# Scores of both context query tiles of a head in one run of matmuls, in the halves of two PSUM banks

## The chip, the cores and the metric

One NeuronCore of a Trainium2 chip runs the whole program. The metric is device time in microseconds of one execution, as the median of several runs. Engines are named as in the profile: PE is TensorE (PEld its weight loads), DVE is VectorE, ACT is ScalarE, POOL is GpSimd, SP is SyncE, which issues the large transfers.

## The reference

Two layers work on 256 latent tokens and 256 context tokens of width 2048. Each layer projects both streams with one wide matrix, runs differential attention and a chunked gating MLP side by side, merges them under sigmoid gates and projects the result. The part that matters here is the attention, with 8 heads, two score maps m per head, and 64 elements in each query and key:

```python
def _pair_attend(q, k, v):
    s = jnp.einsum('bqhmd,bkhmd->bhmqk', q, k).astype(jnp.float32) * (A_QK_DIM ** -0.5)
    p = jax.nn.softmax(s, axis=-1).astype(v.dtype)
    return jnp.einsum('bhmqk,bkhe->bqhme', p, v)
```

The latent queries attend to all 512 keys. The context queries attend to the 256 context keys only, and only in the first of the two layers, since the last layer's context output is not used.

## The kernel before

All matrices are multiplied in three passes of a high and a low part (`mm3`), so each float32 product is three matmuls. The tokens are four tiles of 128: tiles 0 and 1 are context, 2 and 3 latent. The large work is a sequence of chunks of 512 output columns (`tok_chunk`, `tok_steps`, line 315). A chunk loops over pairs of 128 input rows, inside over the token tiles, and each tile has its own PSUM bank of the four tagged `mm`. At the end of a chunk each tile's bank is copied out by a small task, which needs a `w2` buffer first (seven of them, 128 x 512), and the next chunk's first matmul needs a bank that has been copied out.

Everything else runs as Python generators that are interleaved with the chunks when the program is built. The builder keeps a clock of its own (`now`) and the times at which buffers come free (`pool`), and after every few large matmuls it calls `tick` (line 195). `tick` goes through the tasks in the order in which they were made and lets each go on whose request is met: `pe=1` asks for PE (one such step in a tick), `ms=2` for two of the four small PSUM banks, `w2=2` for two buffers, `cond` for a condition. The order that comes out is kept on every engine (lines 47 and 48 for DVE, ACT and POOL, line 231 for matmuls, line 238 for transposes), so most rows of the profile carry one of these three lines. The semaphores behind it are made by the framework, which keeps two engines from touching one PSUM bank at once.

Attention is one task per head and side, `attend` (line 849). `sd == 1` is the latent side with 512 keys, `sd == 0` the context side with 256. Each task takes two query tiles q one after the other. For a tile it asks for two `ms` banks and computes two 128 x nkt score maps with six matmuls: three passes, each over both maps, where map 0 contracts over partitions 0 to 63 and map 1 over partitions 64 to 127. Then come two maxima on DVE, two exponentials on ACT, after each of which a bank is given back, the weighted difference on DVE, a transposition through another `ms` bank and the split into high and low. After both tiles the product with the values is taken (6 matmuls on the context side, 12 on the latent side), in turn (`done["turn"]`, line 904). The counter `done["s"]` (lines 857 and 858) makes the score runs of all tasks come in one fixed order: latent tile 0, latent tile 1, context tile 0, context tile 1, then the next head. So a head's first score run cannot start before the second context run of the head before it was made. The tasks of a pair of heads are made behind the chunk with its queries and keys (lines 1059 to 1066); its two `s8` buffers are given back with the last context run of the pair (line 867).

Of the kernel before, what the change touches and what calls it, by code (L numbers as in the profile page):

```python
# [16 lines left out]
P = 128  # L17
# [4 lines left out]
QKD = 64  # L22
# [340 lines left out]
def dit_kernel(ctx, tc, x, c, ctxt, c_ctx, w_ada, b_ada, norm_g, w_in, q_norm_g, k_norm_g,  # L363
# [3 lines left out]
    B = Builder(ctx, tc)  # L367
# [380 lines left out]
    def layer(L, xt, xn_ev, x_in=None):  # L748
        last = L == DEPTH - 1
# [97 lines left out]
        done = {"n": 0, "turn": 0, "s": 0}  # L847

        def attend(st, vbox, hd, sd, order):
            i = hd % 2  # L850
            es = slice((hd % 4) * P, (hd % 4 + 1) * P)
            vs = slice(i * P, (i + 1) * P)
            nk = 4 if sd == 1 else 2
            nkt = nk * P
            ds = []
            for q in range(2):
                yield dict(pe=1, ms=2, w2=2, cond=lambda: st["n"] == 4 and done["s"] == 2 * order + q)
                done["s"] += 1
                qq, kk = st["qk"]
                ts = slice((2 * sd + q) * P, (2 * sd + q + 1) * P)  # L860
                S = [B.ms()[:, :nkt] for _ in range(2)]
                for a, b in ((0, 0), (0, 1), (1, 0)):
                    for m in range(2):
                        ms_ = slice(m * QKD, (m + 1) * QKD)
                        B.matmul(S[m], qq[ms_, a, i, ts], kk[ms_, b, i, 0:nkt], a + b == 0, a == 1)
                if q == 1 and i == 1 and (sd == 0 or last):
                    B.rel("s8", 2)
                nm = B.st()
                sm = B.st()
                Ps = []  # L870
                for m in range(2):
                    yield
                    V.tensor_reduce(out=nm[:, m:m + 1], in_=S[m], axis=AX.X, op=ALU.max, negate=True)
                for m in range(2):
                    yield
                    p = B.w2()
                    A.activation(out=p[:, :nkt], in_=S[m], func=AF.Exp, bias=nm[:, m:m + 1], scale=1.0,
                                 accum_out=sm[:, m:m + 1])
                    B.rel("ms")
                    Ps.append(p)  # L880
                yield
                rc = B.st()
                V.reciprocal(out=rc[:, 0:2], in_=sm[:, 0:2])
                V.tensor_tensor(out=rc[:, 1:2], in0=rc[:, 1:2], in1=nlam[:, L:L + 1], op=ALU.mult)
                V.tensor_scalar(out=Ps[1][:, :nkt], in0=Ps[1][:, :nkt], scalar1=rc[:, 1:2], scalar2=None, op0=ALU.mult)
                yield
                V.scalar_tensor_tensor(out=Ps[0][:, :nkt], in0=Ps[0][:, :nkt], scalar=rc[:, 0:1], in1=Ps[1][:, :nkt],
                                       op0=ALU.mult, op1=ALU.add)
                B.rel("w2")
                ds.append(Ps[0])  # L890
                if q == 0:
                    yield dict(pe=1, ms=1, cond=lambda: done["turn"] == order and vbox["n"] == 4,
                               **(dict(ws=2) if sd == 1 else dict(w2=2)))
                    dt = [B.t("ws" if sd == 1 else "w2", [P, nk, 256], F32R) for _ in range(2)]
                else:
                    yield dict(pe=1, ms=1)
                pt = B.transpose4([ds[q][:, b * P:(b + 1) * P] for b in range(nk)])
                B.rel("w2")
                yield
                qs = slice(q * P, (q + 1) * P)  # L900
                yield from B.hl(dt[0][:, :, qs], dt[1][:, :, qs], pt[:, :nkt].rearrange("p (b q) -> p b q", q=P))
                B.rel("ms")
            yield dict(pe=1, ms=1, w2=1)
            done["turn"] += 1
            v = vbox["v"][(hd // 2) % 2]
            po = B.ms()
            for kt in range(nk):
                B.mm3(po[:, 0:256], v[:, 0, kt, vs], v[:, 1, kt, vs], dt[0][:, kt], dt[1][:, kt], kt == 0, kt == nk - 1)
            B.rel("ws" if sd == 1 else "w2", 2)
            if i == 1 and (sd == 0 or last):  # L910
                B.rel("s8")
            yield
            dT = B.w2()
            A.copy(out=dT[:, 0:256], in_=po[:, 0:256])
            B.rel("ms")
            yield dict(pe=1, ms=1, **(dict(s8=1) if dn[hd // 4] is None else {}))
            if dn[hd // 4] is None:
                dn[hd // 4] = B.t("s8", [P, nq, 512])
            pq = B.transpose4([dT[:, 0:P], dT[:, P:2 * P]])
            yield  # L920
            ssd = B.st()
            for q in range(2):
                A.activation(out=dT[:, 256 + q * P:256 + (q + 1) * P], in_=pq[:, q * P:(q + 1) * P], func=AF.Square,
                             accum_out=ssd[:, q:q + 1])
            B.rel("w2")
            yield
            box = []
            yield from B.rstd(box, ssd[:, 0:2], 2, P)
            for q in range(2):
                V.tensor_scalar(out=dn[hd // 4][:, 2 * sd + q - q0, es], in0=pq[:, q * P:(q + 1) * P],  # L930
                                scalar1=box[0][:, q:q + 1], scalar2=None, op0=ALU.mult)
            B.rel("ms")
            done["n"] += 1
# [3 lines left out]
        def spawn_pair(st, vbox, p):  # L937
            nonlocal nunit
            for hd in (2 * p, 2 * p + 1):
                for sd in ((1,) if last else (1, 0)):  # L940
                    B.spawn(attend(st, vbox, hd, sd, nunit))
                    nunit += 1
# [540 lines left out]
```

## Time and profile before

| what | value |
|---|---|
| median of 3 runs | 2314.8 us (2314.11 to 2315.73) |
| the profiled execution, its own time | 2314.04 us |
| its span, first to last instruction | 2312.3 us |
| PE busy | 2271.8 us (98%), 10730 matmuls |
| DVE busy | 1487.3 us (64%) |
| ACT busy | 881.1 us (38%) |
| HBM traffic | 377.04 MB read, 5.24 MB written |
| TensorE clock granted, mean | 1.000 |

Busy times are unions of the intervals of an engine's instructions. A matmul's interval reaches past the start of the next one, so what a matmul costs is read from the distance between two starts and not from its duration. Windows are in microseconds from the span's start. In a timeline, neighbouring instructions of one kind are merged into one row with their count.

### The profile page before, as it was taken

Reading aid. Unit: us, or ns where it says so; the run is one execution under the profiler, and the core shown is the slowest. Engines: PE = TensorE matmul, PEld = TensorE weight load, DVE = VectorE, ACT = ScalarE, POOL = GpSimd, SP = SyncE. Lnnn points to the kernel's source line nnn. Section 1 sums busy time; section 2 is a strip of 40 time slices with the busy share of each in tenths; the row PEclk is TensorE's granted clock in tenths of the full one; section 3 lists DMA queues with packets and bytes.
Section 4 is the critical chain, followed back from the end, with each engine's and each line's share of the span. In section 5 each row is a group of like instructions: output and inputs, shape, how many; then the busy total and the mean of one; then the engine's idle time right before and its main releaser. Section 6 shows DMA issues by size and latency. Waiting matters only on the chain.

```text
span 2312.3 us, 28445 instructions
## 1 busy us (share of the span) xinstructions
PE 2271.8 (98%) x10730; PEld 1834.7 (79%) x10730; DVE 1487.3 (64%) x2343; ACT 881.1 (38%) x1387; POOL 112.7 (5%) x119
## 2 busy tenths in 40 slices
PE   4999999999999999999999999999999999999999
PEld 1577777778888888878888888888888888888887
DVE  3456666664446667687766766877757766677655
ACT  3234444452332212223222322554545554444443
POOL 2010111110000000000000000000201000000000
PEclk9999999999999999999999999999999999999999
DMA  9952222333335555555555566654334567777765
GB/s 330 351 174 73 82 74 73 87 92 106 99 91 166 160 157 165 171 167 166 172 160 157 157 206 196 188 162 130 100 92 140 171 186 247 256 252 255 251 201 182
DMA packets 230649, 384.15 MB, mean 166 GB/s; under 512 B 14446, under 2 KB 80080, under 8 KB 229744
## 3 DMA queue, kind: packets, MB, share of 16 engines
q1 hardware_dynamic: 228640, 377.56, 52.4%
q0 software_dynamic: 1872, 4.78, 0.9%
q8 instruction: 84, 1.38, 0.2%
q14 instruction: 53, 0.43, 0.1%
HBM read 377.04 MB, written 5.24 MB: 165 GB/s over the span
## 4 chain that ended last, share of the span: by engine, by line
PE 95%; DMA 3%; DVE 1%; ACT 0%; issue 0%; SPq 0%; DVEq 0%; ACTq 0%
PE mm L231 87%; PE ms L231 4%; PE ms L238 3%; DMA s<-in_w_ada_dram 1%; DMA raw<-in_w_ada_dram 1%; DMA s<-in_x_dram 1%; DVE wl L47 0%; DMA raw<-in_w_in_dram 0%; DMA ws<-in_w_ada_dram 0%; DVE ws L47 0%; DVE w L47 0%; ACT w L47 0%; DVE s L47 0%; DVE x L47 0%; SPq L275 0%
## 5 line engine op out<-in xcount | busy, mean ns | idle before, releaser
L231 PE MATMUL mm<-wh,x 128*128 128x512 f32 (+1 forms) x4352 | 1378.6, 389 | 1.3 <-DVE w L47 1.0
L231 PEld LDWEIGHTS mm<-wh,x 128*128 128x128 f32 x4352 | 810.0, 188 | 189.7 <-issue 30.2
L47 DVE TENSOR_TENSOR wl<-raw,wh 128x1024 fp32r<-128x1024 f32 x496 | 606.6, 1223 | 457.6 <-ACT wh L47 456.1
L47 ACT CAST wh<-raw 128x1024 fp32r<-128x1024 f32 x496 | 521.3, 1052 | 920.0 <-PE mm L231 677.9
L231 PE MATMUL mm<-wl,x 128*128 128x512 f32 (+1 forms) x2176 | 835.2, 384 | 1.2 <-DVE wl L47 1.2
L231 PEld LDWEIGHTS mm<-wl,x 128*128 128x128 f32 x2176 | 409.8, 188 | 74.5 <-DVE wl L47 2.0
L231 PE MATMUL mm<-x,wh 128*128 128x512 f32 x1024 | 316.1, 390 | 0.0
L47 DVE SCALAR_TENSOR_TENSOR ws<-raw,c,ws 128x512 f32<-128x512 f32 x420 | 288.2, 747 | 13.7 <-DMA raw<-in_w_ada_dram 13.0
L231 PEld LDWEIGHTS mm<-x,wh 128*128 128x128 f32 x1024 | 191.7, 188 | 39.9
L231 PE MATMUL mm<-x,wl 128*128 128x512 f32 x512 | 199.5, 390 | 0.0
L231 PE MATMUL mm<-s,wh 128*128 128x512 f32 x512 | 157.8, 389 | 0.0
L47 POOL TENSOR_TENSOR st<-st,c 128x8 f32<-128x8 f32 (+3 forms) x76 | 91.3, 1208 | 877.5 <-DVE st L47 875.6
L231 PEld LDWEIGHTS mm<-x,wl 128*128 128x128 f32 x512 | 96.1, 188 | 20.1
L231 PEld LDWEIGHTS mm<-s,wh 128*128 128x128 f32 x512 | 96.1, 188 | 20.1
L47 DVE TENSOR_REDUCE st<-ms 128x1 f32<-128x512 f32 (+2 forms) x104 | 56.0, 566 | 71.8 <-PE ms L238 40.9
L231 PE MATMUL mm<-s,wl 128*128 128x512 f32 x256 | 99.8, 390 | 0.9 <-DVE wl L47 0.9
L231 PE MATMUL ms<-s,s 64*128 64x512 f32 (+2 forms) x412 | 72.6, 461 | 18.1 <-DVE st L47 12.7
L238 PE MATMUL ms<-c,w 128*128 128x128 f32 (+1 forms) x466 | 74.4, 273 | 13.0 <-DMA w<-in_k_norm_g_dram 6.6
L238 PEld LDWEIGHTS ms<-c,w 128*128 128x128 f32 (+1 forms) x466 | 57.4, 141 | 32.5 <-issue 6.8
L231 PE MATMUL mm<-wh,s 128*128 128x512 f32 x256 | 81.6, 391 | 0.0
L47 ACT ACTIVATE w<-mm 128x512 f32<-128x512 f32 x72 | 43.0, 598 | 98.9 <-PE mm L231 98.8
L47 ACT ACTIVATE w<-ms,st 128x512 f32<-128x512 f32 (+1 forms) x96 | 58.6, 616 | 50.5 <-DVE st L47 50.5
(112 smaller groups left out, 1335.3 us busy)
## 6 DMA issues: line engine op xcount, KB each, us to landing
raw<-in_w_in_dram SPq DMA_DIRECT2D x296, 512.0 KB, 4.0
raw<-in_w_ada_dram SPq DMA_DIRECT2D x128, 512.0 KB, 4.5
raw<-in_w_out_dram SPq DMA_DIRECT2D x72, 512.0 KB, 4.4
raw<-in_w_in_dram SPq DMA_DIRECT2D x128, 256.0 KB, 3.0
raw<-in_w_proj_b_dram SPq DMA_DIRECT2D x32, 512.0 KB, 4.6
raw<-in_w_proj_a_dram SPq DMA_DIRECT2D x32, 512.0 KB, 4.5
s<-in_w_ada_dram SPq DMA_DIRECT2D x62, 256.0 KB, 6.0
raw<-in_w_ada_dram SPq DMA_DIRECT2D x38, 256.0 KB, 6.0
```

The costliest lines, as they stand in the source:

```text
L47: ins = getattr(self.eng, name)(**kw)
L231: self.tc.keep_in_program_order(self.nc.tensor.matmul(out=out, lhsT=lhsT, rhs=rhs, start=start, stop=stop))
L238: self.tc.keep_in_program_order(self.nc.tensor.transpose(out=out, in_=in_, identity=identity))
```

## The change

On the context side (`sd == 0`) the request for PE and two banks is made once. All twelve score matmuls of both query tiles are issued without a break: the six of tile 0 into the first 256 columns of the two banks, then the six of tile 1 into the last 256. The score counter goes up by two at that point, and the `s8` buffers of the pair are given back there. For tile 1 only the request for two `w2` buffers is left, which needs no PE. The banks are given back after the exponentials of tile 1 alone. The latent side issues what it did.

```diff
             ds = []
+            both = sd == 0
             for q in range(2):
-                yield dict(pe=1, ms=2, w2=2, cond=lambda: st["n"] == 4 and done["s"] == 2 * order + q)
-                done["s"] += 1
-                qq, kk = st["qk"]
-                ts = slice((2 * sd + q) * P, (2 * sd + q + 1) * P)
-                S = [B.ms()[:, :nkt] for _ in range(2)]
-                for a, b in ((0, 0), (0, 1), (1, 0)):
-                    for m in range(2):
-                        ms_ = slice(m * QKD, (m + 1) * QKD)
-                        B.matmul(S[m], qq[ms_, a, i, ts], kk[ms_, b, i, 0:nkt], a + b == 0, a == 1)
-                if q == 1 and i == 1 and (sd == 0 or last):
-                    B.rel("s8", 2)
+                if both and q == 1:
+                    yield dict(w2=2)
+                else:
+                    yield dict(pe=1, ms=2, w2=2, cond=lambda: st["n"] == 4 and done["s"] == 2 * order + q)
+                    qq, kk = st["qk"]
+                    banks = [B.ms() for _ in range(2)]
+                    qs_ = (0, 1) if both else (q,)
+                    done["s"] += len(qs_)
+                    for q_ in qs_:
+                        ts = slice((2 * sd + q_) * P, (2 * sd + q_ + 1) * P)
+                        ks = slice(q_ * nkt, q_ * nkt + nkt) if both else slice(0, nkt)
+                        for a, b in ((0, 0), (0, 1), (1, 0)):
+                            for m in range(2):
+                                ms_ = slice(m * QKD, (m + 1) * QKD)
+                                B.matmul(banks[m][:, ks], qq[ms_, a, i, ts], kk[ms_, b, i, 0:nkt], a + b == 0, a == 1)
+                    if qs_[-1] == 1 and i == 1 and (sd == 0 or last):
+                        B.rel("s8", 2)
+                S = [b_[:, q * nkt:q * nkt + nkt] if both else b_[:, :nkt] for b_ in banks]
                 nm = B.st()
...
-                    B.rel("ms")
+                    if q == 1 or not both:
+                        B.rel("ms")
                     Ps.append(p)
```

## Rows read from the trace of the kernel before

**Rows 1.** The page's head, and part 4: the chain of work that ended last, by engine.
```profile
span 2312.3 us, 28445 instructions
...
PE 95%; DMA 3%; DVE 1%; ACT 0%; issue 0%; SPq 0%; DVEq 0%; ACTq 0%
```
**Rows 2.** Busy by window: length, PE, PEld, DVE, ACT, POOL, clock, DMA share, GB/s.
```profile
160.00:260.00 100.00, 100.00 (x499) 79.64 (x498) 69.36 (x152) 44.36 (x104) 11.37 (x9) 1.00 0.27 83
...
360.00:460.00 100.00, 99.88 (x503) 79.37 (x502) 63.23 (x137) 46.67 (x112) 12.87 (x11) 1.00 0.27 77
```
**Rows 3.** PE's waits of windows 560:1480 and 1480:2280: us in total, times, longest.
```profile
PE mm L231 <- DVE wl L47: 2.1, 3, 0.9
PE mm L231 <- DVE w L47: 1.0, 1, 1.0
...
PE ms L238 <- DVE s L47: 1.3, 1, 1.3
```
**Rows 4.** PE's groups by form, whole span: score matmuls with 512 and with 256 keys.
```profile
L231 PE MATMUL ms<-s,s 64*128 64x512 f32 x192 | 30.9, 426 | 0.0
...
L231 PE MATMUL ms<-s,s 64*128 64x256 f32 x96 | 9.9, 313 | 0.0
```
**Rows 5.** Timeline of PE around one context score run: start us, interval us, instruction.
```profile
238.88 0.39 PE L231 MATMUL mm<-wh,x 128*128 128x512 f32 x1
239.20 0.62 PE L231 MATMUL ms<-s,s 64*128 64x256 f32 x6
239.75 0.50 PE L231 MATMUL mm<-wh,x 128*128 128x512 f32 x1
240.09 0.40 PE L231 MATMUL mm<-wl,x 128*128 128x512 f32 x1
240.33 0.39 PE L231 MATMUL mm<-wh,x 128*128 128x512 f32 x1
```
**Rows 6.** The same around one latent score run.
```profile
264.08 0.39 PE L231 MATMUL mm<-wh,x 128*128 128x512 f32 x1
264.39 0.97 PE L231 MATMUL ms<-s,s 64*128 64x512 f32 x6
265.29 0.50 PE L231 MATMUL mm<-wh,x 128*128 128x512 f32 x1
265.63 0.40 PE L231 MATMUL mm<-wl,x 128*128 128x512 f32 x1
265.86 0.39 PE L231 MATMUL mm<-wh,x 128*128 128x512 f32 x1
```
**Rows 7.** The same around a product of probabilities and values (12 matmuls of 256 columns).
```profile
330.66 0.39 PE L231 MATMUL mm<-wl,x 128*128 128x512 f32 x1
330.89 0.40 PE L231 MATMUL mm<-wh,x 128*128 128x512 f32 x1
331.12 1.59 PE L231 MATMUL ms<-ws,s 128*128 128x256 f32 x12
332.54 0.40 PE L231 MATMUL mm<-wh,x 128*128 128x512 f32 x1
```
**Rows 8.** Timeline of PE: both context runs of head 0, first latent run of head 1.
```profile
191.53 0.62 PE L231 MATMUL ms<-s,s 64*128 64x256 f32 x6
...
205.64 0.62 PE L231 MATMUL ms<-s,s 64*128 64x256 f32 x6
...
207.09 0.98 PE L231 MATMUL ms<-s,s 64*128 64x512 f32 x6
```
**Rows 9.** Timeline of ACT: the last exponential of each of these two context runs.
```profile
194.21 0.48 ACT L47 ACTIVATE w<-ms,st 128x256 f32<-128x256 f32 x1
...
207.22 0.47 ACT L47 ACTIVATE w<-ms,st 128x256 f32<-128x256 f32 x1
```
**Rows 10.** Timeline at a chunk's end, all engines: a bank copied out, the load behind it.
```profile
456.78 1.22 ACT L47 COPY w<-mm 128x512 f32<-128x512 f32 x2
...
457.42 0.19 PEld L231 LDWEIGHTS mm<-wh,x 128*128 128x128 f32 x1 [0.54 <-ACT w L47]
```

## The prediction

> **What bounds the kernel now.** I read the page's head and its chain first: 95% of the chain that ended last is PE [rows 1]. So the question of this change is what it does to the time that PE needs for its own sequence, and whether it makes PE wait. Next, busy time by window over the stretch from 160 to 560 us, where layer 0 does its attention: of its four windows of 100 us three show PE busy for 100.00, and the lowest, from 360 to 460, for 99.88, at a granted clock of 1.00 (the 2.4 GHz level), while DVE has 63 to 69 us and ACT 44 to 47 [rows 2]. There is no idle time to win here; PE can only be given less to do, or be made to wait. Then PE's waits: from 560 us on they are a handful, all on DVE, the largest groups 2.1, 1.0 and 1.3 us [rows 3]. A gain made at 200 to 500 us is therefore not eaten by a transfer or another engine later; it should reach the end.
>
> The groups by form say how much there is of the edited work: 96 score matmuls with 256 keys, all in layer 0, that is 16 runs of six, two for each of 8 heads [rows 4]. The 192 with 512 keys are the latent side of both layers, which issues what it did. Their busy time (9.9 us for the 96) is not their cost, since intervals overlap; the timeline around one run gives that.
>
> **What a run costs.** Take the distance between starts. From the large matmul at 238.88 to the one at 240.33 lie 1.45 us, in which three large matmuls (238.88, 239.75, 240.09) and six scores were issued [rows 5]. An undisturbed large matmul takes 0.23 us: two take the 0.46 from 330.66 to 331.12 [rows 7]. So 1.45 - 3 x 0.23 = 0.76 us for six scores. The latent run, with the same number of matmuls and weight loads but twice the columns: 264.08 to 265.86 is 1.78, less 0.69 is 1.09 us [rows 6]. The maps of one pass contract over different halves of the partitions and run side by side, so a run is three pairs; three times 256 more columns cost 1.09 - 0.76 = 0.33, or 0.11 us per 256. Three pairs at 0.11 are 0.33 of the context run's 0.76, and the other 0.43 us is paid once per run: the first score starts 0.32 after a large matmul instead of 0.23, the next large matmul takes 0.34 instead of 0.23 (239.75 to 240.09), and the rest is inside the run [rows 5].
>
> **The change part by part.**
>
> *Sixteen runs of six become eight of twelve.* The number of matmuls, columns and weight loads stays; eight times, the part that is paid per run goes. What three more pairs cost in a run that has begun, no row shows. The nearest is a row of twelve 256-column matmuls, each with weights of its own: 331.12 to 332.54, 1.42/12 = 0.118 us each [rows 7]. I take 0.118 per pair, because that row has the columns and changes its weights as often per column streamed. A run of twelve is then 0.76 + 3 x 0.118 = 1.11 us, against 2 x 0.76 = 1.52: 0.41 saved per head, 8 x 0.41 = **3.3 us**. One bound is 0.11 per pair, from the latent run: 0.43 per head, 3.4 us. The other: the added six cost the whole 0.55 us that six take from their first start to the next large matmul (239.20 to 239.75 [rows 5]), so that only what lies outside that is saved: 0.76 - 0.55 = 0.21 per head, 1.7 us. Beyond that lies only a run of twelve that costs as much as two runs, a gain of zero; nothing in the edit adds a matmul, so I exclude a loss from this part.
>
> *Less planning of PE steps.* The builder lets one PE step go per tick, so the two runs were always apart: 14.1 us for head 0 (191.53 and 205.64 [rows 8]). No second explanation is needed for the 0.43 being paid twice.
>
> *Tile 0's maxima wait for the whole run.* Engines are kept off a bank that PE is writing, so DVE's first maximum comes about 3 x 0.118 = 0.35 us later. Behind it in DVE's queue stand the subtractions that make `wl`, and PE reads those; in this stretch PE waited for none [rows 2], and DVE is idle a third of it. Cost zero, with that slack as the cover; without it, 0.35 us per head, 2.8 us in all.
>
> *Tile 1 needs no PE step for its scores.* Its maxima can start as soon as tile 0 is split, so the context side's chain is shorter by the wait for a turn on PE. That is off the path.
>
> *Two banks are held longer.* Before, a context tile held two banks from its score run to its second exponential: 191.53 to 194.21 + 0.48 = 194.69, 3.2 us, and again from 205.64 to 207.69 [rows 8, 9]. Now they are held from the first point to about the last, some 16 us without a break, and the other tasks have two `ms` banks in that time. What these tasks do (transpositions, products, a score run that needs both) is asked for by the builder only when it thinks a bank is free, so a shortage moves them back and large matmuls go first. Cost on PE zero, as long as there are large matmuls to put there, and PE is full with them all through the stretch [rows 2].
>
> *The next head's score run may go 14 us sooner.* `done["s"]` now allows it right behind the context run instead of after 205.64 (it came at 207.09 [rows 8]). It then takes two `w2` buffers while the head before still needs its own. No instruction is added, but this is the place where the change could bite; see the third rival.
>
> *Buffers of a pair come back sooner,* by the same 14 us. No PE wait in this stretch is for them, so it is worth nothing.
>
> The sum: 2314.04 us, the profiled execution's own time (span 2312.3 and 1.7 around it), less 3.3 is 2310.7. That execution lies 0.76 us under the median of the three runs, 2314.8, so I put the forecast on the median: 2314.8 - 3.3 = **2311.5 us**. About 0.2% (4.6 us) is what a measurement of this kernel can tell from no change, and 3.3 us is 0.14%, inside it.
>
> **The rivals.**
>
> *The added pairs pay for their weight loads.* If a new pair cannot load while the pair before it streams, the added six cost up to their 0.55 us, and the gain is 1.7 us: 2313.1. For it: the context run takes 0.55 for three pairs, 0.18 each, well over 0.11. Against it: that 0.55 holds the start and the end of the run, and the latent run, with as many loads, is longer by columns alone. The Trainium skill (TensorE: Matmul & The Clock Gate, What overlaps and what doesn't, and LDWEIGHTS) has a rule that speaks for this rival: a weight load overlaps running matmuls only if they use another group of rows, and takes columns/1.2 ns. By it a pair would be about 107 + 107 = 213 ns, as an estimate from that page, the run of twelve 0.76 + 0.64 and the gain 1.0 us. The trace does not agree for every pair, since three at 0.213 would not fit in the 0.55 us that three take [rows 5].
>
> *The waits behind it fall otherwise.* The builder derives the order of DVE and ACT anew from the first moved step on, and PE's waits on DVE after 560 us sum to about 4.4 us in [rows 3]. They hang on which DVE instruction stands ahead of which. If at least 1.3 us of them go as well, the change is faster by over 4.6: with half gone 2314.8 - 3.3 - 2.2 = 2309.3, with all 2307.1. If they grow by half, 2313.7. For it: all are single waits of about a microsecond, which a shift of one instruction makes or removes. Against: nothing in the edit aims at them.
>
> *PE waits at a chunk's end, and the kernel is slower.* A chunk's first matmul needs a bank copied out, and the copy needs a `w2` buffer. The trace has one such place within the stretch: the copy at 456.78, and the weight load behind it, idle 0.54 us until ACT's copy was done [rows 10]. The other three tiles' last 18 large matmuls, 18 x 0.23 = 4.1 us, cover a copy. With the next head's scores 14.1 us sooner, `w2` buffers are taken earlier and may be missing when four banks want to be copied. If a copy starts more than about 3.5 us late (4.1 less 0.6 for the copy itself), PE stands: at worst 14 - 4 = 10 us at one chunk's end. One such makes 2311.5 + 10 = 2321.5; it decides from 7.9 us in all, the 3.3 and the 4.6. Against it: the request for scores still asks for two free buffers, tile 1 is quicker through, and only one of the chunk ends in the stretch shows a wait now, of a fraction of a microsecond.
>
> **How the numbers follow.** Forecast as it stands, within a microsecond or so: 0.52. Weight loads paid: 0.12. Later waits smaller by enough: 0.22; larger, but still within 4.6 us of the old time: 0.06. Slower at a chunk's end: 0.08. Faster by over 0.2% (under 2310.2) takes the 0.22 and 0.03 of the forecast's own spread, where 3.4 meets a lucky microsecond: 0.25. Slower by over 0.2% (over 2319.4) is the last, 0.08; the rest, 0.67, lies within. The range reaches down to 2307.5, with nearly all of the waits gone, and up to 2316.0, a gain of 1 us and grown waits of 2; the slow rival and the far end of the fast one are left out.
>
> **What would show it.** The timeline should have eight context runs of 12, each followed by the next large matmul about 0.9 us after its first score (0.55 + 3 x 0.118), with one 0.34 step behind it; 16 runs of six, or a distance near 1.1 us, would refute the size. The windows from 160 to 560 should stay at 100 of 100 for PE, and the products of layer 0 should come 3 us earlier after 560. A new wait of PE on ACT `w` or on a copy in 160 to 560 us would be the slow rival; PE's waits after 560 on DVE `wl`, `w` and `s` decide the second.

## The result and the profile after

The changed kernel takes 2326.37 us (median of 5 runs, 2324.56 to 2329.47) against 2314.80 (2313.76 to 2315.73): a ratio of 1.0053, 95% interval 1.0041 to 1.0064. It is slower by 11.6 us where a gain of 3.3 was forecast, and it lies above the stated range. The ratios, here and below, are given as measured with their intervals; they differ from the quotients of the medians by up to 0.0003.

Head and chain of its page, to be held against [rows 1]:

```profile
span 2323.6 us, 28442 instructions
...
PE 94%; DMA 3%; DVE 2%; ACT 1%; issue 0%; SPq 0%; POOL 0%; ACTq 0%; DVEq 0%; POOLq 0%
```

PE's share of the chain is a percent lower, those of DVE and ACT are a percent higher each: PE now waits for them somewhere. Busy time by window over the stretch with layer 0's attention (columns as in [rows 2]) says where:

```profile
160.00:260.00 100.00, 99.88 (x500) 80.11 (x499) 66.84 (x146) 43.63 (x103) 11.47 (x9) 1.00 0.26 81
260.00:360.00 100.00, 96.48 (x483) 76.48 (x482) 63.66 (x139) 46.94 (x111) 9.36 (x8) 0.98 0.25 74
360.00:460.00 100.00, 99.46 (x508) 78.21 (x507) 63.34 (x136) 45.08 (x107) 10.33 (x9) 1.00 0.27 80
460.00:560.00 100.00, 95.28 (x445) 77.24 (x444) 55.91 (x108) 43.30 (x88) 9.62 (x11) 0.97 0.31 93
```

Before, PE was full here [rows 2]. Now 8.9 of 400 us are missing, nearly all in the second and the fourth window, and there the granted clock is under 1 as well. PE's waits of the changed kernel from 160 to 560 us:

```profile
PE mm L231 <- ACT w L47: 5.1, 4, 2.3
PE ms L238 <- DVE w L47: 3.1, 1, 3.1
PE ms L238 <- ACT w L47: 0.5, 1, 0.5
```

From 560 to 1480 us the waits are those of before [rows 3] to the digit:

```profile
PE mm L231 <- DVE wl L47: 2.1, 3, 0.9
PE mm L231 <- DVE w L47: 1.0, 1, 1.0
```

So from 160 us on the waits that were added all lie where layer 0's attention ran. `mm <- ACT w` is a large matmul that waits for ACT to copy a bank out into a `w2` buffer, which is the place that the third rival named. ACT's copies at the chunk end near 450 us, in the kernel before:

```profile
449.26 0.59 ACT L47 COPY w<-mm 128x512 f32<-128x512 f32 x1
450.43 0.57 ACT L47 COPY w<-mm 128x512 f32<-128x512 f32 x1
```

The third and fourth came at 456.78 [rows 10]. In the changed kernel:

```profile
453.32 0.59 ACT L47 COPY w<-mm 128x512 f32<-128x512 f32 x1 [0.47 <-PE mm L231]
459.01 0.58 ACT L47 COPY w<-mm 128x512 f32<-128x512 f32 x1
464.90 0.57 ACT L47 COPY w<-mm 128x512 f32<-128x512 f32 x1
470.16 0.59 ACT L47 COPY w<-mm 128x512 f32<-128x512 f32 x1
```

Four banks that took 8.7 us to empty (449.26 to 458.00) now take 17.4, with 5 to 6 us between copies of 0.6 us. PE at the same place, and at the earlier chunk end near 295 us:

```profile
294.09 0.60 PE L238 MATMUL ms<-c,w 128*128 128x128 f32 x4
297.78 1.08 PE L238 MATMUL ms<-c,w 128*128 128x128 f32 x4 [3.09 <-DVE w L47]
298.51 0.77 PE L231 MATMUL mm<-wh,x 128*128 128x512 f32 x1
299.09 0.63 PE L231 MATMUL mm<-wl,x 128*128 128x512 f32 x1
299.51 1.05 PE L231 MATMUL mm<-wh,x 128*128 128x512 f32 x2
...
467.39 0.63 PE L231 MATMUL mm<-wl,x 128*128 128x512 f32 x1
467.82 0.63 PE L231 MATMUL mm<-wh,x 128*128 128x512 f32 x1
470.80 0.50 PE L231 MATMUL mm<-wh,x 128*128 128x512 f32 x1 [2.34 <-ACT w L47]
```

The matmul at 470.80 starts 0.05 us after the copy at 470.16 has ended. The wait of 3.09 us is a transposition's, for DVE, but it lies at a chunk's end too: the last copy there starts at 296.12, and the next large matmul comes at 298.51. The rows also show a second loss: behind the wait of 3.09 us that ends at 297.78 (299.09 to 299.51), and again in the second stretch (467.39 to 467.82), large matmuls stand 0.42 to 0.43 us apart in place of 0.23. The windows give the clock of both stretches:

```profile
298.00:301.00 3.00, 3.00 (x10) 2.51 (x10) 1.74 (x5) 0.95 (x2) 0.48 (x1) 0.50 0.00 0
465.00:475.00 10.00, 7.13 (x18) 5.18 (x19) 7.74 (x18) 6.22 (x10) 2.83 (x3) 0.67 0.00 1
```

A clock of 0.50 is the lower of the two levels, 1.2 GHz, and PE fell to it behind waits of 2 to 3 us. Each such slow matmul costs 0.2 us more. How much that is in all can be estimated from the granted clock of the second and the fourth window above: 100 x (0.02 + 0.03), about 5 us. With the 8.7 us of waits that makes some 13.7 of the 14.9 us to be explained (the 11.6 lost and the 3.3 that should have been saved).

The saved entries are there too. One context run of the changed kernel, to be held against [rows 5]:

```profile
191.29 0.39 PE L231 MATMUL mm<-wh,x 128*128 128x512 f32 x1
191.61 0.98 PE L231 MATMUL ms<-s,s 64*128 64x256 f32 x12
192.52 0.50 PE L231 MATMUL mm<-wh,x 128*128 128x512 f32 x1
192.86 0.40 PE L231 MATMUL mm<-wl,x 128*128 128x512 f32 x1
193.09 0.62 PE L231 MATMUL mm<-wh,x 128*128 128x512 f32 x2
```

From 191.29 to 193.09 are 1.80 us; less three large matmuls, 0.69, the twelve cost 1.11 us, as forecast.

### The profile page after: what moved, and what is told of

Read it like the earlier page. It is cut to its first block, busy times and chain, and to the rows that moved or that the text cites. A ratio compares the mean times of both kernels' runs of the same rounds, so it can differ in the third digit from the quotient of the medians.

```text
span 2323.6 us, 28442 instructions
## 1 busy us (share of the span) xinstructions
PE 2274.5 (98%) x10730; PEld 1837.9 (79%) x10730; DVE 1487.1 (64%) x2343; ACT 882.0 (38%) x1387; POOL 109.8 (5%) x119
## 4 chain that ended last, share of the span: by engine, by line
PE 94%; DMA 3%; DVE 2%; ACT 1%; issue 0%; SPq 0%; POOL 0%; ACTq 0%; DVEq 0%; POOLq 0%
PE mm L231 87%; PE ms L231 4%; PE ms L238 3%; DMA s<-in_w_ada_dram 1%; DMA raw<-in_w_ada_dram 1%; DMA s<-in_x_dram 1%; DVE wl L47 0%; ACT w L47 0%; DMA ws<-in_w_ada_dram 0%; DVE s L47 0%; DVE w L47 0%; DMA raw<-in_w_in_dram 0%; DVE ws L47 0%; POOL st L47 0%; DVE x L47 0%
```

## The experiments

All edits below leave the arithmetic as it is; they change requests, banks or buffers, and with them the order of the work. Each interval reaches some 2 us to either side, so a difference of 1 to 3 us between two experiments rests on the waits in their traces more than on their times.

Three theories were set against each other first. Theory 1: two causes together. The context run holds two of the four small PSUM banks for long, and the next head's latent run, which may now follow it at once, takes the other two; small tasks that wait for a bank sit on their `w2` buffers, and the copies find none. Theory 2: the early run alone, by the two buffers it takes. Theory 3: the long hold of the banks alone.

**The merged run without the early run** (`e1_turn`). The counter that admits the next head goes up by its second step only when tile 1 goes on:

```diff
                 if both and q == 1:
                     yield dict(w2=2)
+                    done["s"] += 1
...
-                    done["s"] += len(qs_)
+                    done["s"] += 1
```

> The merged run as in the change, but the score counter goes up by one with it and by the second one only when context tile 1 goes on, so the next head's first latent run keeps the place it had. Theory 1 (banks and the early run together: the context run holds two ms banks for some 16 us, the next head's run takes the other two at once, the small tasks then sit on their w2 buffers waiting for a bank, and the copies at a chunk's end get none): no wait of PE over 1 us from 160 to 560 us, 2311 to 2313 us, the 3.3 us of saved entries kept. Theory 2 (the early run alone, by its w2 buffers): the same here. Theory 3 (the long hold of the banks alone): as slow as the change, 2322 to 2328 us.

Measured: 2312.93 us (11 runs) against 2314.82 (33 runs), ratio 0.9991, interval 0.9982 to 1.0000. From 160 to 560 us PE's waits are one row:

```profile
PE mm L231 <- ACT w L47: 0.8, 2, 0.6
```

With the early run taken away, the merged run is faster by 1.9 us, with an interval from 0 to 4.2, so the 3.3 us may be there in full or in part. Theory 3 falls: the banks are held across both tiles here as well.

**The hold alone** (`e6_hold`), from the changed kernel: two runs of six in their old places, tile 1 in the second half of the banks that tile 0 took, all given back after tile 1:

```diff
-                if both and q == 1:
-                    yield dict(w2=2)
-                else:
-                    yield dict(pe=1, ms=2, w2=2, cond=lambda: st["n"] == 4 and done["s"] == 2 * order + q)
+                if True:
+                    yield dict(pe=1, w2=2, cond=lambda: st["n"] == 4 and done["s"] == 2 * order + q,
+                               **({} if both and q == 1 else dict(ms=2)))
...
-                    banks = [B.ms() for _ in range(2)]
-                    qs_ = (0, 1) if both else (q,)
+                    if not (both and q == 1):
+                        banks = [B.ms() for _ in range(2)]
+                    qs_ = (q,)
```

> The banks are held as in the change, both context tiles in the halves of the same two banks, given back after tile 1, but the two score runs of six stay apart and in their old places. Theory 1 and theory 2: the time of before within 1 us, 2314 to 2316. Theory 3: the waits of the change without its saving, 2325 to 2331 us.

Measured: 2315.85 us against 2314.82, ratio 1.0002, interval 0.9993 to 1.0011: the time of before within the interval, and no wait of PE is listed from 160 to 560 us. Holding the banks costs nothing that can be seen as long as the next head's run stays in its old place.

**The early run alone** (`e4_early`), in the kernel before:

```diff
-                yield dict(pe=1, ms=2, w2=2, cond=lambda: st["n"] == 4 and done["s"] == 2 * order + q)
-                done["s"] += 1
+                yield dict(pe=1, ms=2, w2=2, cond=lambda: st["n"] == 4 and (done["s"] == 2 * order + q or (sd == 0 and q == 1)))
+                done["s"] += (1 if sd else 2 - 2 * q)
```

> The kernel before, two runs and own banks, but the score counter goes up by two with context tile 0, so the next head's first latent run may come before context tile 1 as it may in the change. Theory 1: part of the waits, since no bank is held long: 2315 to 2320 us. Theory 2: all of the waits of the change and none of its saving, 2327 to 2331 us. Theory 3: the time of before, 2314 to 2316 us.

Measured: 2317.66 us, ratio 1.0009, interval 1.0000 to 1.0018, so 2.8 us slower by the medians. PE waits for copies here too, in 160 to 560 us:

```profile
PE mm L231 <- ACT w L47: 2.4, 2, 1.6
```

The early run alone makes the same kind of wait, but a fifth of the 14.9 us. Theory 2 falls as a full account.

**The change, with one bank left free** (`e8_bank`). A head's first latent run asks for three free banks and takes two:

```diff
-                    yield dict(pe=1, ms=2, w2=2, cond=lambda: st["n"] == 4 and done["s"] == 2 * order + q)
+                    yield dict(pe=1, ms=3 if sd == 1 and q == 0 else 2, w2=2, cond=lambda: st["n"] == 4 and done["s"] == 2 * order + q)
+                    if sd == 1 and q == 0:
+                        B.cur[2] = B.now
+                        B.rel("ms")
```

> The change, with one thing more: a head's first latent run is asked for only when three ms banks are free, takes two and leaves one to the small tasks. Theory 1: no wait of PE over 1 us from 160 to 560 us, 2311 to 2313 us. Theory 2: the early run is late here too, so at most part of the waits, 2311 to 2318 us. Theory 3: the banks are held as long as in the change, 2322 to 2328 us.

Measured: 2315.54 us, ratio 1.0003, interval 0.9994 to 1.0012. All 11 us of loss are gone, but no gain is left. The waits from 160 to 560 us are gone (not one is listed), as theory 1 has it, though the time lies outside its range; one new wait stands in layer 1, whose latent runs ask for the third bank as well:

```profile
PE ms L238 <- DMA w<-in_w_spatial_dram: 3.3, 1, 3.3
```

This does not tell theory 1 from theory 2, because the request does more than leave a bank free. While the context run holds two of the four banks, three can't be free, so the next head's run must wait until the first of them comes back: the early run is taken away here as well. The next experiment, with the same request, shows it. Head 0's last exponential, and behind it head 1's first latent run, which came at 207.09 before [rows 8]:

```profile
208.82 0.46 ACT L47 ACTIVATE w<-ms,st 128x256 f32<-128x256 f32 x1
...
209.29 0.97 PE L231 MATMUL ms<-s,s 64*128 64x512 f32 x6
```

**The same in layer 0 only** (`e9_bank_layer0`), the request with `and not last`. By then a fourth theory stood beside the first. In the change tile 1 asks for two `w2` buffers and no longer for PE, so it need not wait for a turn on PE. Theory 4: with the early run, it is this that takes buffers ahead of the copies.

> The change with the request for three free banks ahead of a head's first latent run, as in e8_bank, but in layer 0 alone, so that layer 1 keeps its order. Theory 1 (long hold and early run together starve the small tasks of banks) and theory 4 (early run, and tile 1 going on without a turn on PE, together take the w2 buffers ahead of the copies): both 2311 to 2313 us, no wait of PE over 0.5 us from 160 to 560 us, and no wait of 3.3 us for the spatial weights in layer 1.

Measured: 2311.96 us (11 runs) against 2314.94 (26 runs), ratio 0.9988, interval 0.9979 to 0.9997: 3.0 us faster than before (0.7 to 4.9 by the interval). PE is full again in the windows where the change lost:

```profile
260.00:360.00 100.00, 100.00 (x513) 79.14 (x512) 64.75 (x139) 48.44 (x117) 10.47 (x8) 1.00 0.24 76
...
460.00:560.00 100.00, 100.00 (x483) 81.50 (x482) 61.55 (x112) 44.16 (x88) 9.21 (x9) 1.00 0.32 102
```

**Its control** (`e14_before_bank`): the same request in the kernel before.

> The kernel before with the request for three free banks ahead of a head's first latent run in layer 0, the control of e9_bank_layer0. If what e9_bank_layer0 gained is the eight saved entries: 2314 to 2316 us, the time of before. If the request itself brought it: 2311 to 2313 us.

Measured: 2316.20 us against 2315.41, ratio 1.0005, interval 0.9996 to 1.0014. The request by itself brings nothing, so what `e9_bank_layer0` gained is put down to the eight saved entries.

**Early run and hold, two runs of six** (`e10_hold_early`): `e6_hold`, with the counter up by two at tile 0 and tile 1 free of it.

```diff
-                               cond=lambda: st["n"] == 4 and done["s"] == 2 * order + q,
+                               cond=lambda: st["n"] == 4 and (done["s"] == 2 * order + q or (both and q == 1)),
...
-                    done["s"] += len(qs_)
+                    done["s"] += 2 - 2 * q if both else 1
```

> Two runs of six in the halves of the same two banks, held as long as in the change, and the score counter up by two with tile 0, so the next head's first latent run may come early as in the change. Tile 1 still needs a turn on PE for its six matmuls. Theory 1: the waits of the change without its saving, 2326 to 2331 us. Theory 4: no more than the early run alone cost, 2316 to 2320 us.

Measured: 2321.05 us, ratio 1.0025, interval 1.0015 to 1.0035: 6.1 us slower by the medians, which lies between the two expectations. The waits from 160 to 560 us:

```profile
PE mm L231 <- ACT w L47: 3.0, 2, 2.7
PE ms L238 <- DVE w L47: 0.7, 2, 0.4
```

The hold, free by itself, costs another 3 us once the early run is there. That difference is hardly clear of the two intervals, but the traces agree with it: 3.7 us of waits here, 2.4 in `e4_early`, and a clock of 0.98 in the window from 460 to 560 where `e4_early` has 1.00. So theory 1's pair seems real; but it makes less than half of the loss.

**The change, with tile 1 waiting for a turn on PE** (`e11_tile1_turn`), one word:

```diff
                 if both and q == 1:
-                    yield dict(w2=2)
+                    yield dict(pe=1, w2=2)
```

> The change, but context tile 1's request for two w2 buffers asks for a turn on PE as well, though it uses none. Banks are held as long and the next head's run may come as early as in the change. Theory 1: as slow as the change, 2322 to 2328 us. Theory 4: only the waits of the early run alone (about 3 us) are left beside the 3.3 us saved, 2313 to 2317 us.

Measured: 2317.24 us, ratio 1.0010, interval 1.0001 to 1.0019. It lies just above what theory 4 gave. That word takes back 9 of the 14.9 us. With the 3.3 us of saved entries put back it stands at 5.6 us over the kernel before, where `e10_hold_early` stands at 6.1. Its waits in the stretch are one row:

```profile
PE mm L231 <- ACT w L47: 4.6, 2, 3.2
```

The time came out nearly as theory 4 has it, but the traces do not show its mechanism. At the first chunk end of the loss, the changed kernel has head 3's first latent run, the first and the last copy, and the first step in which tile 0 of head 2's context side is split into high and low; then head 7's first latent run, in front of the second chunk end:

```profile
281.32 0.97 PE L231 MATMUL ms<-s,s 64*128 64x512 f32 x6
283.22 0.59 ACT L47 COPY w<-mm 128x512 f32<-128x512 f32 x1 [0.47 <-PE mm L231]
296.12 0.58 ACT L47 COPY w<-mm 128x512 f32<-128x512 f32 x1
306.38 0.37 ACT L47 CAST w<-ms 128x256 fp32r<-128x256 f32 x1 [3.95 <-PE ms L238]
...
451.43 0.97 PE L231 MATMUL ms<-s,s 64*128 64x512 f32 x6
```

In the program tile 1 asks for its buffers only behind that split, so it held none of them while the copies waited. The two latent runs came at these times in the kernel before:

```profile
307.64 0.96 PE L231 MATMUL ms<-s,s 64*128 64x512 f32 x6
...
482.79 0.98 PE L231 MATMUL ms<-s,s 64*128 64x512 f32 x6
```

and in `e11_tile1_turn` at these:

```profile
309.01 0.97 PE L231 MATMUL ms<-s,s 64*128 64x512 f32 x6
...
444.32 0.97 PE L231 MATMUL ms<-s,s 64*128 64x512 f32 x6
```

So the word moved the first of them behind the copies, and the waits there are gone; the second still stands in front of them, and both waits of the row above lie there. The word's 9 us come mainly from where the run lands. (In `try_step` a request with `pe=1` also loses a lead of 300 ns and is not held back by a backlog on DVE or ACT, so the word changes three rules of the builder at once.)

**Eight `w2` buffers** (`e12_w2_8`), the change with `w2=8, st=24` for `w2=7, st=40`, in the table of buffers and in the builder's pool.

> The change with eight w2 buffers in place of seven, the room taken from the small st tiles (24 in place of 40). Theory 1: banks are as short as before, so at least half of the waits stay, 2318 to 2326 us. Theory 4: the w2 buffers are what the copies wait for, so most of the waits go, 2311 to 2316 us.

Measured: 2342.24 us, ratio 1.0118, interval 1.0104 to 1.0132, far from both. Another number of buffers gives the whole program another order, so a control was needed: the kernel before with the same buffers.

> The kernel before with the buffers of e12_w2_8 (eight w2, 24 st), as its control. If the loss of e12_w2_8 behind 560 us comes from the change: 2314 to 2317 us. If it comes from the other number of buffers, which gives another order to the whole program: 2335 to 2345 us, with the same waits behind 560 us, and then the two differ by the 3.3 us saved and by what waits there are from 160 to 560 us.

Measured: 2345.69 us, ratio 1.0130, interval 1.0113 to 1.0147. So the loss behind 560 us belongs to the buffers. PE's waits from 560 to 1480 us, `e12_w2_8` first:

```profile
PE mm L231 <- DVE wl L47: 6.5, 4, 3.7
PE mm L231 <- DVE w L47: 6.0, 2, 5.0
PE mm L231 <- DVE s L47: 3.7, 1, 3.7
...
```

and `e13_before_w2_8`, where the other rows are the same:

```profile
...
PE mm L231 <- DVE s L47: 2.8, 1, 2.8
...
```

Within the pair the change is 3.4 us faster by the medians (2342.24 against 2345.69), which is not clear of the two intervals, some 3 us to either side each. The waits from 160 to 560 us, again `e12_w2_8` and then the control:

```profile
PE mm L231 <- ACT w L47: 2.0, 2, 1.6
```

```profile
PE mm L231 <- ACT w L47: 1.4, 1, 1.4
PE ms L238 <- DVE w L47: 0.4, 1, 0.4
```

With one buffer more, and banks as short as in the change, the change adds 0.2 us of waits (2.0 against 1.8) where it added 8.7 with seven. That points to the `w2` buffers as what the copies went without, though the order of the whole program is another one too.

**Where the next head's run lands.** The traces of all kernels can be held against each other at the two chunk ends of the loss, near 285 and near 455 us. The table has how long before the first copy the next head's first latent run starts, and what PE waits there, both in us:

| kernel | `w2` buffers | run ahead, 285 | waits | run ahead, 455 | waits |
|---|---|---|---|---|---|
| the change | 7 | 1.9 | 3.5 | 1.9 | 5.1 |
| `e11_tile1_turn` | 7 | behind the copies | 0 | 4.3 | 4.6 |
| `e10_hold_early` | 7 | 10.2 | 1.0 | 10.2 | 2.7 |
| `e4_early` | 7 | 11.1 | 0 | 11.1 | 2.4 |
| `e14_before_bank` | 7 | among the copies | 0.9 | behind | 0.2 |
| before, `e1_turn`, `e6_hold`, `e8_bank`, `e9_bank_layer0` | 7 | behind | 0 | behind | 0.2 at most |
| `e12_w2_8` | 8 | 10.7 | 0.3 | 10.7 | 1.6 |
| `e13_before_w2_8` | 8 | 1.9 | 0 | 1.9 | 1.8 |

With seven buffers, PE waits for more than 0.2 us at these places only where that run stands in front of the copies or among them, and at the second end the longer the nearer in front it stands. With eight, the same distance of 1.9 us costs 1.8 us at both ends together, in place of 8.7. By the program the run takes two `w2` buffers and keeps one of them until its head's turn.

## Why the prediction was wrong

*What bounds the kernel, and the price of a run*: right. PE's sequence was the path, and a run of twelve costs the 1.11 us that were forecast. The three added pairs took 0.91 - 0.55 = 0.36 us (191.61 to 192.52, against [rows 5]), or 0.12 each. So the first rival fell. The estimate of 0.213 us for a pair from the Trainium skill (TensorE: Matmul & The Clock Gate, What overlaps and what doesn't, and LDWEIGHTS) does not agree with these 0.12 us. Where no wait covers it, the gain is 3.0 us (`e9_bank_layer0`, 0.7 to 4.9 by its interval), as the sum had it.

*Waits behind 560 us*: unchanged; the second rival had no part.

*The step that failed* is "The next head's score run may go 14 us sooner". I saw the place, put nothing for it into the sum, and gave it as a rival with up to 10 us for one chunk end and a chance of 0.08. The 14.1 us are head 0's, which is far from a chunk's end. At the two chunk ends of the loss the run went 26 and 31 us sooner (281.32 for 307.64, 451.43 for 482.79) and landed 1.9 us ahead of the copies, and PE waited 3.5 and 5.1 us there. Where the run is put back (`e1_turn`, `e9_bank_layer0`), the loss is gone. By itself the early run costs 2.8 us (`e4_early`).

*Two more steps made it larger.* "Two banks are held longer" had "Cost on PE zero": true alone (`e6_hold`), but about 3 us with the early run (6.1 in `e10_hold_early`, less 2.8). The cover that I named, large matmuls that go first, was not there when it mattered, since at a chunk's end the large matmuls themselves wait for a small task, the copy. "Tile 1 needs no PE step for its scores" was to make the context side's chain shorter, and "off the path". With the early run ahead of it the chain became longer, and so did the hold. Head 0's last exponential, which ended at 207.69 before, in the changed kernel:

```profile
213.71 0.46 ACT L47 ACTIVATE w<-ms,st 128x256 f32<-128x256 f32 x1
```

The banks are held for 22.6 us from 191.61 on, not for some 16; in `e9_bank_layer0`, without the early run, it is 16.5. Giving tile 1 its request for PE back takes 9 us away (`e11_tile1_turn`), mainly by moving one of the two latent runs behind the copies; so the three steps do not add up one by one, and I had costed them one by one. Together they are 14.9 us.

*The third rival* named the place rightly, and its price for one chunk end was of the right order. It left out that there are two such ends and that the clock falls: the waits sum to 8.7 us, and behind those of 2 to 3 us the large matmuls ran at the lower level, about 5 us more in all.

*A reading that was too narrow*: over the four windows from 160 to 560 us DVE has 60 to 69 us and ACT 44 to 48, not 63 to 69 and 44 to 47. Nothing hung on it.

*What stays open.* The trace does not record which task held which `w2` buffer when a copy had none. That the copies lacked buffers rests on the two kernels with eight of them, and that the run's two were the missing ones on the program and on the table. How the word in `e11_tile1_turn` moved the run was not followed through the builder. Why the same run makes more waits the nearer it stands to the copies was not tested by itself, and about 1 of the 14.9 us is not found.

## What to carry to other kernels

A condition that comes true earlier is a change as much as an instruction that is no longer issued: ask which task now goes ahead, what it takes from a shared pool, and what stands right behind it. Price the edits that share a pool together, and at every place where the bounding engine itself depends on that pool (here the copies at each chunk's end), not by the average cover or by the first head. A merge that is sound on its engine can be kept by giving it back the old order around it: with the next head's run held back by its request for three free banks in layer 0, it runs in 2311.96 us against 2314.94.

## What was not expected of the hardware

One wait of 3.09 us of an engine that is otherwise nearly full was followed by a granted clock of 0.50: 298 to 301 us shows it throughout. I had priced only the wait.
